# A hybrid decoder trunk on one core: probabilities and the state space output transposed by VectorE in place and by transfers that land in the same tile, with longer steps

## The chip, the core and the metric

The kernel runs on one core of a Trainium2 chip. Its engines work side by side, each through its own instructions in order: TensorE (PE, matmuls and their weight loads PEld), VectorE (DVE), ScalarE (ACT), GpSimd (POOL) and SyncE (SP, which here issues nearly all transfers). The metric is the device time of one execution in microseconds, lower is better. Matmul operands lie in SBUF, results land in PSUM.

## What is computed

Two layers, each: a feed-forward block, a mixer with three branches, a second feed-forward block, on 256 tokens of width 1024 in float32. Cut to what matters here:

```python
def swiglu_ffn(x, w_gu, w_down):                 # FFN_HIDDEN = 2816
    gate, up = jnp.split(x @ w_gu, 2, axis=-1)
    return (jax.nn.silu(gate) * up) @ w_down

def hybrid_mixer(xn, ...):
    q, k, v, z, xbc, dt_raw, u, vg, gate_raw = jnp.split(xn @ w_in, split_at, axis=-1)
    y_a = moba_attention(q, k, v)                # at 256 tokens: causal softmax attention, 8 heads x 128, ALiBi
    y_s = ssd_scan(xs, dt, a, bm, cm) + d_skip[:, None] * xs      # 16 heads x 64, 2 chunks of 128 tokens
    y_s = rms_norm(y_s.reshape(b_, s, SSM_WIDTH) * jax.nn.silu(z), ssm_norm_g)
    y_c = u * spatial_gating(vg)
    merged = gates[:, :, 0] * (y_a @ p_attn) + gates[:, :, 1] * (y_s @ p_ssm) + gates[:, :, 2] * (y_c @ p_sgu)
    return merged @ w_out
...
    h = h + 0.5 * rms_norm(swiglu_ffn(rms_norm(h, g), ...), g2)   # before and after the mixer
```

## The kernel before, in words

**Matmuls.** Every float32 product is made of three matmuls on split operands (hi and lo parts): `x_hi w_hi`, `x_hi w_lo`, `x_lo w_hi` (`unit`, lines 213 to 215). I call these three a triple; one has 512 columns. Weights come in 495 blocks of 128x1024 (512 KB). SP loads a block into one of six `raw` buffers (L160), ScalarE casts it to `whi` (L180), VectorE subtracts to get `wlo` (L181); eleven split pairs are kept. The two tiles of 128 tokens (t = 0, 1) use each block in turn, and a block is two triples wide, so a *step* is two triples and a block is two steps.

**The order.** The order of all instructions is written out by the Python program. After each step `pump` (L198) counts 1.3 off the waiting time of every spawned task, in the order in which they were spawned, lets those that have come to zero go on to their next `yield`, and then emits the next weight split if one is due. The waits stand in the table `W` (L48). A task's wait of 1.3 is one step, one of 5.2 counts down to a tiny positive remainder and takes five, and a wait of 0 lasts until the next step. `finish` lets a task run to its end at once.

**Transposes.** A product needs its left operand with features on partitions. Three ways are in use. `T.transpose` on TensorE, four 128x128 tiles into one PSUM buffer of the tag `tr` (three buffers, `TR`): tokens of q and k (`transposed`, L513, tile `ctr`), the state space output y (`to_parts`, L300, tile `xtr`, then times the gain on VectorE, `xg`, L314) and the probabilities (`attention`, L787, tile `ptr`, copied by ScalarE to `pT`, L789). In the feed-forward part `swap_out` transposes 32x32 squares on VectorE into another tile (L277), writes it to DRAM in one transfer, and `swap_in` reads it back in four transfers that gather pieces of 512 bytes into a third tile `hr` (L286); `evac` waits `W["out"]` between writing and reading and `W["in"]` before it uses the result.

**The mixer around the change.** Projections run in the order xbc, z, q, k, v, gate 1 and the product with `p_ssm`, vg, gate 0 and the product with `p_attn`, u, gate 2 and so on; each half of 512 columns is eight steps. `ssd` (L651) is spawned before the second half of q. For each token tile t and group g it makes decay weights for two sets of four heads: `weights(t, q)` (L676) is one matmul into PSUM (`seg`), a mask added on VectorE (`ssw`, L682), four exponentials on ScalarE (L686), a product on VectorE (L688). `scaled(t)` (L665) starts y on GpSimd (L668) and scales xs on VectorE (L671). Then come the matmuls `yd` (L711), the sum and product into y on VectorE (L714, L722), and at the end of a tile the sum of squares of y on ScalarE (`junk`, L270) and, after `W["ys"]`, `to_parts`. `qk_evac` copies a finished half of q or k from PSUM to `qtok` on ScalarE (L504), waits `W["qk"]` and transposes it on TensorE (`ctr`). `attention` (L746) computes scores and probabilities of one token tile for 8 heads (tiles `sc`), transposes them after `W["p1"]` and multiplies them with v after `W["p3"]` (`pv`, L796). The `branch` product waits for its operand's task by `finish(*need)`.

Of the kernel before, what the change touches and what calls it, by code (L numbers as in the profile page):

```python
# [44 lines left out]
ACC, TR = 5, 3  # L45


W = {'gw': 6.5, 'tr': 0, 'parts': 0, 'sq': 1.3, 'lead': 3.9, 'sq2': 5.2, 'hh': 5.2, 'x0': 0.65, 'cv': 5.2, 'cs': 6.5, 'xs': 0, 'dt1': 2.6, 'dt2': 0, 'dt3': 5.2, 'cb': 2.6, 'w1': 1.3, 'w2': 5.2, 'ys': 3.9, 'qk': 3.9, 'vv': 0, 'qs': 0, 'ex': 0, 'p1': 10.4, 'p2': 0, 'p3': 3.9, 'ge': 0, 'ln': 10.4, 'sv': 0, 'yc': 9.1, 'mg': 3.9, 'out': 6.5, 'in': 6.5}  # L48


@with_exitstack
def trunk(ctx, tc, a):
# [219 lines left out]

    def swap_out(src, w):
        xt = b2("xt")
        V.transpose(xt[:, :w], src[:, :w])  # L277
        rd = dram.tile([P, w], F32, name=f"swap{w}", tag=f"swap{w}", bufs=8)
        nc.sync.dma_start(rd, xt[:, :w])
        return rd  # L280

    def swap_in(dst, rd):

        v = rd.rearrange("(a i) (c e) -> c i a e", a=4, c=4)
        for c in range(4):
            nc.sync.dma_start(dst[32 * c:32 * c + 32], v[c])  # L286

    def halves(ps, hi, lo):

# [105 lines left out]
    def ffn(x, r2, nxt, head=HOLD):  # L395
# [3 lines left out]
        def evac(c, w, gate, up):  # L399
            silu, hh = {}, {}  # L400
            for t in range(NT):
                while gate(t) is None:
                    yield 0
                silu[t] = b2("silu")
                A.activation(silu[t][:, :w], gate(t), AF.Silu, scale=r2[t])  # L405
            for t in range(NT):
                while up(t) is None:
                    yield 0
                hh[t] = b2("hh")
                V.scalar_tensor_tensor(hh[t][:, :w], up(t), r2[t], silu[t][:, :w], op0=ALU.mult, op1=ALU.mult)  # L410
            n = w // P
            rd = {t: swap_out(hh[t], w) for t in range(NT)}
            yield W["out"]
            hr = {}
            for t in range(NT):
                hr[t] = b2("hr")
                swap_in(hr[t][:, :w].rearrange("p (a e) -> p a e", a=4), rd[t])
            yield W["in"]
            new = b4 if n > 2 else b2
            hT[c] = (new("hTh", (P, NT, n, P), F32R), new("hTl", (P, NT, n, P), F32R))  # L420
            for t in range(NT):
                hi, lo = (z[:, t].rearrange("p k (a j) -> p a k j", a=4) for z in hT[c])
                r4 = hr[t][:, :w].rearrange("p (a k j) -> p a k j", a=4, k=n)
# [54 lines left out]
    def mixer(l, x, r2, nxt):  # L478
# [169 lines left out]

        h3 = lambda q, n=SH: q.rearrange("p (h e) -> p h e", h=n)

        def ssd(ysx, rs):  # L651
            bT = lambda g, t: bc["T"][:, g, t * P:(t + 1) * P]
            cT = lambda g, t: bc["T"][:, 2 + g, t * P:(t + 1) * P]
# [38 lines left out]
            for t in range(NT):  # L692
# [53 lines left out]
        def attention(yax, free):  # L746
            for t in range(NT):
                while t and not free:
                    yield 0
                n = (t + 1) * P  # L750
                per = 512 // n
                sc = {}
                mx = small("mx", NH)
                for g in range(2):
                    sc[g] = (b4 if t else b2)("sc", (P, 4, n))
                    for u in range(0, 4, per):
                        ps = tr("qk")
                        for j in range(per):
                            hh = u + j
                            T.matmul(ps[:, j * n:(j + 1) * n], qk["q", g][:, hh, t * P:(t + 1) * P],  # L760
                                     qk["k", g][:, hh, 0:n], start=True, stop=True)
                        for j in range(per):
                            hh = u + j
                            V.scalar_tensor_tensor(sc[g][:, hh, :], alibi[t], 2.0 ** -(4 * g + hh + 1),
                                                   ps[:, j * n:(j + 1) * n], op0=ALU.mult, op1=ALU.add)
                        yield W["qs"]
                    V.reduce_max(mx[:, 4 * g:4 * g + 4], sc[g], axis=AX.X)
                nmx = small("nmx", NH)
                V.tensor_scalar(nmx, mx, -1.0, None, op0=ALU.mult)
                den = small("den", NH)  # L770
                for g in range(2):
                    for j in range(4):
                        c = slice(4 * g + j, 4 * g + j + 1)
                        A.activation(sc[g][:, j, :], sc[g][:, j, :], AF.Exp, bias=nmx[:, c], accum_out=den[:, c])
                    yield W["ex"]
                rden = small("rden", NH)
                V.reciprocal(rden, den)
                for g in range(2):
                    V.tensor_tensor(sc[g], sc[g], rden[:, 4 * g:4 * g + 4, None].to_broadcast([P, 4, n]), op=ALU.mult)
                hi, lo = yax.new(t)  # L780
                for g in range(2):
                    yield W["p1"]
                    pts = {}
                    for k in range(t + 1):
                        pt = tr("ptr")
                        for j in range(4):
                            T.transpose(pt[:, j * P:(j + 1) * P], sc[g][:, j, k * P:(k + 1) * P], ident)  # L787
                        pts[k] = b2("pT", (P, 4, P))
                        A.copy(pts[k], pt.rearrange("p (h q) -> p h q", h=4))  # L789
                        yield W["p2"]  # L790
                    yield W["p3"]
                    po = tr("pv")
                    for j in range(4):
                        hh = 4 * g + j
                        for k in range(t + 1):
                            T.matmul(po[:, j * P:(j + 1) * P], vv[k][:, hh * HD:(hh + 1) * HD], pts[k][:, j, :],  # L796
                                     start=k == 0, stop=k == t)
                    halves(po, hi[:, 4 * g:4 * g + 4, :], lo[:, 4 * g:4 * g + 4, :])


        uu, vg = {}, {}
# [285 lines left out]
def _arrays(i):  # L1087
# [4 lines left out]
    order = [xbc, z, q, k, v, g1, f["p_ssm"], vg, g0, f["p_attn"], u, g2, f["p_sgu"], f["w_out"]]  # L1092
    mix = [_chunks(m).reshape(L, -1, P, 1024) for m in order]
    col = lambda m: m.reshape(L, -1, P).transpose(0, 2, 1)
    par = np.concatenate(
        [col(f["ffn1_pre_g"]), col(f["mix_pre_g"]), col(f["ffn2_pre_g"]), col(f["ssm_norm_g"]),
         f["conv_w"].reshape(L, 4, CT, P).transpose(0, 3, 2, 1).reshape(L, P, 48),
         col(f["conv_b"]), f["sgu_b"].transpose(0, 2, 1)], axis=2)
    return {
# [35 lines left out]
```

## Time and profile before

| what | value |
|---|---|
| median of 3 runs | 1486.92 us (1486.62 to 1488.68) |
| the profiled execution, its own time | 1487.98 us |
| its span, first to last instruction | 1486.2 us |
| TensorE busy | 1472.1 us (99%) |
| VectorE busy | 955.2 us (64%) |
| ScalarE busy | 782.6 us (53%) |
| GpSimd busy | 55.6 us (4%) |
| mean granted TensorE clock | 0.997 |

Busy time is the time in which an engine had an instruction at work; matmuls are pipelined, so the duration of one (about 0.39 us) is longer than the time it adds to a run of them (0.23 us). "Idle before" is the time an engine sat still before an instruction, with the instruction that released it. The granted clock is the share of full speed (2.4 GHz) that TensorE got. Times inside a trace count from the span's start; the two layers show the same pattern some 734.5 us apart, and rows of layer 0 are shown.

### The profile page before, as it was taken

The page shows a single profiled execution, that of the slowest core. Times are in us where ns is not written, and L with a number is a line of the kernel's source. Part 1 is how long each engine was busy: PE and PEld are TensorE (multiplying, and loading weights), DVE is VectorE, ACT ScalarE, POOL GpSimd, SP SyncE. Part 2 cuts the span into 40 slices and gives each one's busy share as a digit, 9 for nine tenths or more (in the row PEclk, how much of TensorE's full clock was granted, in tenths as well). Part 3 has the DMA queues.
Part 4 walks back from the last instruction along what each step waited for, and adds up shares of the span by engine and source line. Part 5 has one row for each costly group of instructions (what it writes and reads, how often), then busy time and mean ns, then how long its engine had stood idle before and what let it go on. Part 6 is the DMA issues. An engine that isn't in the chain of part 4 may idle for free.

```text
span 1486.2 us, 18786 instructions
## 1 busy us (share of the span) xinstructions
PE 1472.1 (99%) x6850; PEld 1218.8 (82%) x6850; DVE 955.2 (64%) x1160; ACT 782.6 (53%) x1079; POOL 55.6 (4%) x98
## 2 busy tenths in 40 slices
PE   9999999999999999999999999999999999999998
PEld 7888888878888888888888888888788888888886
DVE  6766477766666857656486564876665667676652
ACT  6644367555374536544364543765554645464441
POOL 0000020000000000000000000200000000000000
PEclk9999999999999999999999999999999999999999
DMA  8987655335556445888568784654354564478860
GB/s 291 323 253 236 199 190 179 127 115 184 159 181 217 168 154 198 283 230 259 163 230 256 235 253 132 224 167 135 119 192 141 194 204 170 134 272 261 238 200 29
DMA packets 112476, 293.37 MB, mean 197 GB/s; under 512 B 16896, under 2 KB 41600, under 8 KB 112384
## 3 DMA queue, kind: packets, MB, share of 16 engines
q1 hardware_dynamic: 111808, 291.84, 60.6%
q8 instruction: 54, 0.88, 0.2%
q10 hardware_dynamic: 576, 0.33, 0.1%
q14 instruction: 38, 0.31, 0.1%
HBM read 279.54 MB, written 12.58 MB: 197 GB/s over the span
## 4 chain that ended last, share of the span: by engine, by line
PE 94%; DVE 4%; ACT 1%; issue 1%; POOL 0%; DMA 0%; DVEq 0%; ACTq 0%; POOLq 0%
PE gu L213 11%; PE gu L215 11%; PE gu L214 11%; PE dn L213 5%; PE dn L215 5%; PE dn L214 5%; PE br L213 3%; PE br L215 3%; PE br L214 3%; PE gate L215 2%; PE gate L213 2%; PE gate L214 2%; DVE wlo L181 2%; PE xbc L215 1%; PE xbc L213 1%; PE xbc L214 1%
## 5 line engine op out<-in xcount | busy, mean ns | idle before, releaser
L181 DVE TENSOR_TENSOR wlo<-raw,whi 128x1024 fp32r<-128x1024 f32 x495 | 600.2, 1232 | 331.1 <-ACT whi L180 319.8
L180 ACT CAST whi<-raw 128x1024 fp32r<-128x1024 f32 x495 | 512.8, 1051 | 380.9 <-PE gu L215 131.8
L213 PE MATMUL gu<-whi,xh 128*128 128x512 f32 x704 | 276.0, 392 | 1.4 <-ACT xh L316 1.4
L214 PE MATMUL gu<-wlo,xh 128*128 128x512 f32 x704 | 274.9, 391 | 0.0
L215 PE MATMUL gu<-whi,xl 128*128 128x512 f32 x704 | 274.8, 390 | 0.0
L213 PEld LDWEIGHTS gu<-whi,xh 128*128 128x128 f32 x704 | 132.7, 188 | 29.8 <-ACT xh L316 1.8
L215 PEld LDWEIGHTS gu<-whi,xl 128*128 128x128 f32 x704 | 132.6, 188 | 28.0 <-DVE xl L317 0.4
L214 PEld LDWEIGHTS gu<-wlo,xh 128*128 128x128 f32 x704 | 132.5, 188 | 27.9 <-DVE wlo L169 0.9
L213 PE MATMUL dn<-whi,hTh 128*128 128x512 f32 x352 | 137.5, 391 | 0.0
L215 PE MATMUL dn<-whi,hTl 128*128 128x512 f32 x352 | 137.0, 389 | 0.0
L214 PE MATMUL dn<-wlo,hTh 128*128 128x512 f32 x352 | 136.9, 389 | 0.0
L215 PEld LDWEIGHTS dn<-whi,hTl 128*128 128x128 f32 x352 | 66.1, 188 | 13.8
L213 PE MATMUL gate<-whi,xh 128*128 128x512 f32 x192 | 77.3, 403 | 0.0
L214 PEld LDWEIGHTS dn<-wlo,hTh 128*128 128x128 f32 x352 | 66.1, 188 | 13.5
L213 PEld LDWEIGHTS dn<-whi,hTh 128*128 128x128 f32 x352 | 66.1, 188 | 13.4
L215 PE MATMUL gate<-whi,xl 128*128 128x512 f32 x192 | 75.0, 391 | 0.0
L214 PE MATMUL gate<-wlo,xh 128*128 128x512 f32 x192 | 74.8, 390 | 0.0
L316 ACT CAST xh<-xg 128x512 fp32r<-128x512 f32 (+1 forms) x25 | 15.1, 603 | 62.3 <-DVE xg L314 62.3
L215 PEld LDWEIGHTS gate<-whi,xl 128*128 128x128 f32 x192 | 36.0, 188 | 7.7
L405 ACT ACTIVATE silu<-gu,r 128x512 f32<-128x512 f32 (+1 forms) x48 | 31.3, 654 | 19.8 <-PE gu L215 16.2
L214 PEld LDWEIGHTS gate<-wlo,xh 128*128 128x128 f32 x192 | 36.2, 188 | 6.6
L213 PEld LDWEIGHTS gate<-whi,xh 128*128 128x128 f32 x192 | 36.1, 188 | 6.6
(243 smaller groups left out, 2248.3 us busy)
## 6 DMA issues: line engine op xcount, KB each, us to landing
raw<-in_mix SPq DMA_DIRECT2D x232, 512.0 KB, 4.2
raw<-in_gu SPq DMA_DIRECT2D x175, 512.0 KB, 4.9
raw<-in_dn SPq DMA_DIRECT2D x88, 512.0 KB, 4.5
swap<-xt SPq DMA_DIRECT2D x40, 256.0 KB, 3.2
hr<-swap SPq DMA_DIRECT2D x160, 64.0 KB, 4.9
row_ffn_post_g<-in_ffn_post_g SPq DMA_DIRECT2D x4, 512.0 KB, 7.0
swap<-xt SPq DMA_DIRECT2D x8, 128.0 KB, 4.4
hr<-swap SPq DMA_DIRECT2D x32, 32.0 KB, 6.1
```

Source lines behind the costliest of these rows:

```text
L180: A.copy(hi, w)
L181: V.tensor_tensor(lo, w, hi.bitcast(F32), op=ALU.subtract)
L213: T.matmul(o, xh(k, t), hi[:, off:off + n], start=first, stop=False)
L214: T.matmul(o, xh(k, t), lo[:, off:off + n], start=False, stop=False)
L215: T.matmul(o, xl(k, t), hi[:, off:off + n], start=False, stop=last)
L316: A.copy(o_h, xg)
L405: A.activation(silu[t][:, :w], gate(t), AF.Silu, scale=r2[t])
```

## The change

- `swap_out` and `swap_in` give way to `turn` and `land`. `turn` transposes the 32x32 squares in place, then writes to DRAM in four transfers, one per group of 32 partitions, each in pieces (512 bytes; 256 in the chunk of width 256). `land` reads it back in one transfer, whole rows, into the same tile. A transfer of `land` waits for the four writes of its `turn`. The feed-forward part uses them on `hh`; the tiles `xt` and `hr` go.
- The state space output no longer goes through `to_parts`. A task of its own per token tile, `turned`, is spawned with a wait of 1.3 at the tile's end: `turn`, wait `out`, `land`, wait `in`, then gain, cast and subtraction in two halves. `ssd` goes on to the next tile with no wait. `p_ssm` and the gain are stored in the matching order of rows.
- The probabilities are laid out by (32 keys, head, 32 keys) runs: scores are written, reduced, exponentiated and scaled through views of `sc` in runs of 32. `turn` and `land` replace TensorE's transposes and the copies `pT`; between them stand `W["out"]` and then the new `W["pv"]` of 11.7, and `pv` streams `sc` in four runs of 32 columns.
- In `W`, `out` goes from 6.5 to 7.8 and `in` from 6.5 to 9.1, `pv` is new; `ys`, `p1`, `p2`, `p3` are no longer read. `turn_whole` and `land_whole` are added and not called.

```diff
-W = {..., 'ys': 3.9, ..., 'p1': 10.4, 'p2': 0, 'p3': 3.9, ..., 'mg': 3.9, 'out': 6.5, 'in': 6.5}
+W = {..., 'ys': 3.9, ..., 'p1': 10.4, 'p2': 0, 'p3': 3.9, ..., 'mg': 3.9, 'pv': 11.7, 'out': 7.8, 'in': 9.1}
...
+    def turn(src, m, e=128):
+        V.transpose(src, src)
+        rd = dram.tile([m, 4, 32, 4, e], F32, name=f"turn{m}_{e}", tag=f"turn{m}_{e}", bufs=8)
+        for b in range(4):
+            nc.sync.dma_start(rd[:, :, :, b, :].rearrange("m c i e -> i (m c) e"),
+                              src[32 * b:32 * b + 32].rearrange("p (x e) -> p x e", e=e))
         return rd
+    def land(dst, rd):
+        nc.sync.dma_start(dst, rd.rearrange("m c i a e -> (c i) m (a e)"))
...
-            rd = {t: swap_out(hh[t], w) for t in range(NT)}
+            rd = {t: turn(hh[t][:, :w], 1, w // 4) for t in range(NT)}
             yield W["out"]
-            hr = {}
-            for t in range(NT):
-                hr[t] = b2("hr")
-                swap_in(hr[t][:, :w].rearrange("p (a e) -> p a e", a=4), rd[t])
+            for t in range(NT):
+                land(hh[t][:, None, :w], rd[t])
             yield W["in"]
...
+        def turned(t, y, gcol):
+            rd = turn(y, 2)
+            yield W["out"]
+            land(y.rearrange("p (q e) -> p q e", q=2), rd)
+            yield W["in"]
+            new = ysx.new(t)
+            for q in range(2):
+                o_h, o_l = (x[:, 4 * q:4 * q + 4, :].rearrange("p k (a j) -> p a k j", a=4) for x in new)
+                r4 = y[:, 512 * q:512 * q + 512].rearrange("p (a k j) -> p a k j", a=4, k=4)
+                V.tensor_tensor(r4, r4, gcol[:, None, 4 * q:4 * q + 4, None].to_broadcast([P, 4, 4, 32]), op=ALU.mult)
+                A.copy(o_h, r4)
+                V.tensor_tensor(o_l, r4, o_h.bitcast(F32), op=ALU.subtract)
+                yield 0.65
...
                 rs[t] = rsqrt([sumsq(y[t], "sy")], "rs", 1.0 / D)
-                yield W["ys"]
-                yield from to_parts(y[t], *ysx.new(t), gcol=pl[:, G_SSM:G_SSM + 8])
+                yt[t] = spawn(turned(t, y[t], pl[:, G_SSM:G_SSM + 8]), wait=1.3)
...
                 for g in range(2):
-                    V.tensor_tensor(sc[g], sc[g], rden[:, 4 * g:4 * g + 4, None].to_broadcast([P, 4, n]), op=ALU.mult)
+                    V.tensor_tensor(sc[g].rearrange("p (b h j) -> p b h j", h=4, j=32),
+                                    sc[g].rearrange("p (b h j) -> p b h j", h=4, j=32),
+                                    rden[:, None, 4 * g:4 * g + 4, None].to_broadcast([P, 4 * m, 4, 32]), op=ALU.mult)
+                    rd[g] = turn(sc[g], m)
+                    yield 1.3
+                yield W["out"]
+                for g in range(2):
+                    land(sc[g].rearrange("p (m e) -> p m e", m=m), rd[g])
+                yield W["pv"]
                 hi, lo = yax.new(t)
                 for g in range(2):
-                    yield W["p1"]
-                    pts = {}
-                    for k in range(t + 1):
-                        pt = tr("ptr")
-                        for j in range(4):
-                            T.transpose(pt[:, j * P:(j + 1) * P], sc[g][:, j, k * P:(k + 1) * P], ident)
-                        pts[k] = b2("pT", (P, 4, P))
-                        A.copy(pts[k], pt.rearrange("p (h q) -> p h q", h=4))
-                        yield W["p2"]
-                    yield W["p3"]
+                    pts = sc[g].rearrange("p (m a h j) -> p m h a j", m=m, a=4, h=4)
                     po = tr("pv")
...
-        b0 = branch(ysx, rs, [ss], first=True)
+        b0 = branch(ysx, rs, [ss, *yt.values()], first=True)
```

## Rows read from the trace of the kernel before

**Rows 1.** The page's first part: busy time, share of the span and instructions of each engine.

```profile
PE 1472.1 (99%) x6850; PEld 1218.8 (82%) x6850; DVE 955.2 (64%) x1160; ACT 782.6 (53%) x1079; POOL 55.6 (4%) x98
```

**Rows 2.** The page's fourth part: the chain of work that ended last, shares of the span by engine.

```profile
PE 94%; DVE 4%; ACT 1%; issue 1%; POOL 0%; DMA 0%; DVEq 0%; ACTq 0%; POOLq 0%
```

**Rows 3.** Windows of the span, in us from its start: length, then busy time of PE, PEld, DVE, ACT and POOL with their instructions, the granted TensorE clock, the transfers' share and GB/s.

```profile
300.00:315.00 15.00, 12.62 (x57) 9.86 (x56) 10.25 (x11) 7.72 (x14) 2.61 (x3) 0.90 0.29 89
...
400.00:450.00 50.00, 50.00 (x246) 42.02 (x245) 34.12 (x41) 31.22 (x53) 0.00 (x0) 1.00 0.57 190
...
600.00:920.00 320.00, 320.00 (x1422) 265.08 (x1421) 190.81 (x203) 151.47 (x179) 5.08 (x13) 1.00 0.74 231
```

**Rows 4.** What TensorE waited for, over the span: us in total, times, the longest.

```profile
PE ctr L513 <- DVE ssw L682: 3.2, 2, 1.6
PE seg L680 <- DVE xg L314: 1.6, 2, 0.8
```

**Rows 5.** TensorE's timeline in layer 0: start, us, engine, line, operation, tiles, and in brackets the idle time before it and who ended it.

```profile
296.12 1.89 PE L711 MATMUL yd<-xs,ssw 128*128 128x64 f32 x16
297.82 0.48 PE L213 MATMUL k<-whi,xh 128*128 128x512 f32 x1
...
308.72 0.49 PE L680 MATMUL seg<-acsr,sel 128*128 128x512 f32 x1 [0.81 <-DVE xg L314]
310.79 0.63 PE L513 MATMUL ctr<-con,qtok 128*128 128x128 f32 x4 [1.58 <-DVE ssw L682]
...
311.95 0.59 PE L213 MATMUL k<-whi,xh 128*128 128x512 f32 x1
...
315.59 0.39 PE L213 MATMUL k<-whi,xh 128*128 128x512 f32 x1
316.28 0.39 PE L213 MATMUL k<-whi,xh 128*128 128x512 f32 x1
```

**Rows 6.** Windows of one microsecond in that stretch, columns as in rows 3.

```profile
309.00:310.00 1.00, 0.22 (x1) 0.00 (x0) 0.65 (x2) 0.32 (x1) 0.00 (x0) 1.00 0.97 160
...
313.00:314.00 1.00, 1.00 (x3) 0.75 (x3) 1.00 (x2) 0.43 (x1) 0.00 (x0) 0.50 0.00 0
...
315.00:316.00 1.00, 1.00 (x5) 0.82 (x4) 0.62 (x2) 0.34 (x2) 0.00 (x0) 0.80 0.07 4
```

**Rows 7.** TensorE's groups of instructions by line and form over the span: count, busy us, mean ns of one, idle us before them.

```profile
L796 PE MATMUL pv<-pT,v 128*128 128x128 f32 x96 | 12.0, 274 | 0.0
...
L787 PE MATMUL ptr<-con,sc 128*128 128x128 f32 x48 | 7.2, 272 | 0.0
...
L300 PE MATMUL xtr<-con,y 128*128 128x128 f32 x32 | 4.8, 272 | 0.0
```

**Rows 8.** Pieces of the chain that ended last, in order of time: start, us that the piece adds to the chain, engine, tile, line, instructions. There are 8 groups of transposes of y (four per layer) and 12 of the probabilities; one of each is shown, with `yd` and `pv`.

```profile
332.13 1.73 PE yd L711 x16
...
338.91 0.44 PE xtr L300 x4
...
373.42 0.89 PE pv L796 x8
...
1178.22 0.44 PE ptr L787 x4
```

**Rows 9.** Groups of VectorE and ScalarE by line and form: count, busy us, mean ns of one, idle us before them and who ended most of it.

```profile
L277 DVE STREAM_TRANSPOSE xt<-hh 128x512 f32<-128x512 f32 x40 | 25.9, 687 | 0.0
...
L671 DVE TENSOR_TENSOR xs<-xs,dt 128x1024 f32<-128x1024 f32 x4 | 4.9, 1219 | 0.0
...
L424 ACT CAST hTh<-hr 128x512 fp32r<-128x512 f32 x40 | 24.7, 617 | 13.1 <-DMA hr<-swap 12.6 <-issue 0.2
...
L316 ACT CAST xh<-xg 128x512 fp32r<-128x512 f32 x23 | 14.3, 620 | 59.4 <-DVE xg L314 59.4
...
L789 ACT COPY pT<-ptr 128x512 f32<-128x512 f32 x12 | 7.0, 584 | 10.6 <-PE ptr L787 10.6
...
L181 DVE TENSOR_TENSOR wlo<-raw,whi 128x1024 fp32r<-128x1024 f32 x495 | 600.2, 1232 | 331.1 <-ACT whi L180 319.8
```

**Rows 10.** The longest of SP's queue waits over the span: us in total, times, the longest.

```profile
SPq L160 <- DVE wlo L181: 959.2, 416, 17.3
```

**Rows 11.** Transfers by line: count, KB each, median us from issue to landing.

```profile
swap<-xt SPq DMA_DIRECT2D x40, 256.0 KB, 3.2
hr<-swap SPq DMA_DIRECT2D x160, 64.0 KB, 4.9
```

**Rows 12.** Timeline of VectorE, ScalarE and GpSimd at the end of token tile 0 of layer 0, columns as in rows 5.

```profile
298.78 0.69 DVE L722 TENSOR_TENSOR y<-y,zs 128x512 f32<-128x512 f32 x1
...
299.58 1.06 ACT L270 ACTIVATE junk<-y 128x1024 bf16<-128x1024 f32 x1 [3.47 <-DVE y L722]
...
301.58 1.26 ACT L504 ACTIVATE qtok<-k,r 128x512 f32<-128x512 f32 x2
...
301.61 1.90 POOL L668 TENSOR_TENSOR y<-xs,hpar 128x1024 f32<-128x1024 f32 x1
...
301.71 2.89 DVE L181 TENSOR_TENSOR wlo<-raw,whi 128x1024 fp32r<-128x1024 f32 x1 [2.24 <-ACT whi L180]
```

**Rows 13.** ScalarE's exponentials for the first two sets of weights of token tile 0, layer 0, columns as in rows 5.

```profile
275.40 1.28 ACT L686 ACTIVATE ssw<-ssw,nacs 128x128 f32<-128x128 f32 x4 [1.95 <-DVE ssw L682]
...
279.24 1.28 ACT L686 ACTIVATE ssw<-ssw,nacs 128x128 f32<-128x128 f32 x4 [2.08 <-DVE ssw L682]
```

More of the change, by code (lines that the diff above doesn't have):

```diff
@@ L45 @@
 ACC, TR = 5, 3
-W = {'gw': 6.5, 'tr': 0, 'parts': 0, 'sq': 1.3, 'lead': 3.9, 'sq2': 5.2, 'hh': 5.2, 'x0': 0.65, 'cv': 5.2, 'cs': 6.5, 'xs': 0, 'dt1': 2.6, 'dt2': 0, 'dt3': 5.2, 'cb': 2.6, 'w1': 1.3, 'w2': 5.2, 'ys': 3.9, 'qk': 3.9, 'vv': 0, 'qs': 0, 'ex': 0, 'p1': 10.4, 'p2': 0, 'p3': 3.9, 'ge': 0, 'ln': 10.4, 'sv': 0, 'yc': 9.1, 'mg': 3.9, 'out': 6.5, 'in': 6.5}
+W = {'gw': 6.5, 'tr': 0, 'parts': 0, 'sq': 1.3, 'lead': 3.9, 'sq2': 5.2, 'hh': 5.2, 'x0': 0.65, 'cv': 5.2, 'cs': 6.5, 'xs': 0, 'dt1': 2.6, 'dt2': 0, 'dt3': 5.2, 'cb': 2.6, 'w1': 1.3, 'w2': 5.2, 'ys': 3.9, 'qk': 3.9, 'vv': 0, 'qs': 0, 'ex': 0, 'p1': 10.4, 'p2': 0, 'p3': 3.9, 'ge': 0, 'ln': 10.4, 'sv': 0, 'yc': 9.1, 'mg': 3.9, 'pv': 11.7, 'out': 7.8, 'in': 9.1}
 @with_exitstack
@@ L271, in sumsq, with turn_whole, land_whole @@
         return ss
[L275 to L279, printed above, removed]
-        return rd
[L282 to L286, printed above, removed]
+    def turn(src, m, e=128):
[4 more added lines that the diff above has]
+                              src[32 * b:32 * b + 32].rearrange("p (x e) -> p x e", e=e))
+        return rd
+    def land(dst, rd):
+        nc.sync.dma_start(dst, rd.rearrange("m c i a e -> (c i) m (a e)"))
+    def turn_whole(toks):
+        rd = dram.tile([4, P, S], F32, name="turnw", tag="turnw", bufs=6)
+        v = rd.rearrange("k (c i) (t a j) -> t a i (k c) j", c=4, a=4, t=NT)
+        for t in range(NT):
+            V.transpose(toks[t], toks[t])
+            for b in range(4):
+                nc.sync.dma_start(v[t, b], toks[t][32 * b:32 * b + 32, :].rearrange("p (b j) -> p b j", j=32))
+        return rd
+    def land_whole(o, rd):
+        nc.sync.dma_start(o, rd.rearrange("k p e -> p k e"))
     def halves(ps, hi, lo):
@@ L763, in attention @@
                             hh = u + j
-                            V.scalar_tensor_tensor(sc[g][:, hh, :], alibi[t], 2.0 ** -(4 * g + hh + 1),
-                                                   ps[:, j * n:(j + 1) * n], op0=ALU.mult, op1=ALU.add)
+                            V.scalar_tensor_tensor(s4[g][:, hh], alibi[t].rearrange("p (b j) -> p b j", j=32),
+                                                   2.0 ** -(4 * g + hh + 1),
+                                                   ps[:, j * n:(j + 1) * n].rearrange("p (b j) -> p b j", j=32),
+                                                   op0=ALU.mult, op1=ALU.add)
                         yield W["qs"]
-                    V.reduce_max(mx[:, 4 * g:4 * g + 4], sc[g], axis=AX.X)
+                    V.tensor_reduce(mx[:, 4 * g:4 * g + 4], s4[g], axis=AX.XY, op=ALU.max)
                 nmx = small("nmx", NH)
@@ L795, in attention @@
                         for k in range(t + 1):
-                            T.matmul(po[:, j * P:(j + 1) * P], vv[k][:, hh * HD:(hh + 1) * HD], pts[k][:, j, :],
+                            T.matmul(po[:, j * P:(j + 1) * P], vv[k][:, hh * HD:(hh + 1) * HD], pts[:, k, j],
                                      start=k == 0, stop=k == t)
                     halves(po, hi[:, 4 * g:4 * g + 4, :], lo[:, 4 * g:4 * g + 4, :])
+                    yield 1.3
         uu, vg = {}, {}
@@ L1091, in _arrays @@
     q, k, v, z, xbc, dt, u, vg, g0, g1, g2 = (w[:, :, s:e] for s, e in zip(cut[:-1], cut[1:]))
-    order = [xbc, z, q, k, v, g1, f["p_ssm"], vg, g0, f["p_attn"], u, g2, f["p_sgu"], f["w_out"]]
+    weave = lambda m: _woven(np.swapaxes(m, 1, 2), 512).swapaxes(1, 2)
+    order = [xbc, z, q, k, v, g1, weave(f["p_ssm"]), vg, g0, f["p_attn"], u, g2, f["p_sgu"], f["w_out"]]
     mix = [_chunks(m).reshape(L, -1, P, 1024) for m in order]
```

16 lines of the change are left out of this document (10 added, 6 removed).

## The prediction

> **What bounds the kernel now.** I read the page's busy times first: TensorE is busy 1472.1 of 1486.2 us, VectorE 955.2, ScalarE 782.6 [rows 1], and the chain that ended last is 94% TensorE [rows 2]. So a microsecond of TensorE work is a microsecond of the span wherever TensorE has no gap. Then I asked where it has gaps. The windows show 320.00 busy of 320.00 us in the feed-forward stretch and 50.00 of 50.00 in the attention stretch; only 300 to 315 us, inside the mixer, lacks 2.4 us, and its granted clock is 0.90 [rows 3]. TensorE's waits name the culprits, once per layer each: a state space transpose buffer (`ctr` waits for `ssw`, 3.2 us in 2 times; `seg` waits for `xg`, 1.6 us in 2 times) [rows 4]. The timeline shows them at 308.72 (0.81 idle) and 310.79 (1.58 idle); from 311.95 to 315.59 three triples of matmuls take 3.64 us, where one usually takes 0.69 (315.59 to 316.28) [rows 5]. The granted clock is 0.50 there, the lower level (1.2 GHz); it was 1.00 before the two idle gaps and comes back after 315 [rows 6]. 3.64 instead of 2.06 costs 1.6 us. The stretch therefore loses 0.81 + 1.58 + 1.6 = 4.0 us a layer, 8.0 in all.
>
> **Removed from TensorE.** 32 transposes of y and 48 of the probabilities [rows 7] go, in groups of four that take 0.44 us each of the chain [rows 8]: 8 + 12 groups, 20 x 0.44 = **8.8 us off**. TensorE is full there, so this counts whole. Twelve `pT` copies of 584 ns leave ScalarE [rows 9]; nothing of it is on the path.
>
> **Added on VectorE.** Transposes in place: a 512-wide one is 687 ns, and I take 1.22 us for 1024 from the other 1024-wide operation [rows 9]. A layer has two of y (1024), two of 512 and two of 1024 for the probabilities: 6.25 us, 12.5 in all. VectorE is busy 34.12 of 50 us in the attention stretch [rows 3], so this hides behind matmuls; if that cover were gone it would cost 12.5. The new layout in runs of 32 costs nothing that a row shows: ScalarE's cast that gathers such runs (`hTh`) is 617 ns, the plain one (`xh`) 620 [rows 9]. The two groups of PE transposes give their PSUM buffers back to the ring of three.
>
> **The strided moving operand of `pv`.** No row shows one. Nearest: a 64-column `yd` matmul takes as long as a 128-column `pv` one in the chain (1.73 us for 16, 0.89 for 8, both 0.11) [rows 8], so `pv` isn't held by the columns it streams and a slower read has room. It can't gain, as the columns stay. Ends: 0, and 96 [rows 7] x 0.11 = 10.6 us if every one doubled. I take 0, the nearer to that row.
>
> **The transfers.** The feed-forward ones stay ten per chunk, one whole write and four gathers becoming four scattered writes and one whole landing; 60 are new. All go through SP, in order with the weight loads; a landing waits on SP until its four writes are done, and the loads of `raw` queue behind it. SP already spends 959.2 us waiting for VectorE's `wlo` [rows 10], and six raw and eleven split blocks of 2.74 us (two steps) are ahead of TensorE. A scattered write isn't in the trace: 256 KB whole land in 3.2 us, 64 KB in pieces in 4.9 [rows 11]; twice the bytes at most double it, 3.2 to 9.8, and I take 4.9, the row with the same pieces. A step is two triples, 1.37 us. Counting 1.3 off each wait, `out` is now 7 steps (9.6 us), `in` 8 (11.0), `pv` 9 (12.3), so both legs are covered. In the feed-forward part `out` plus `in` grow from 12 to 15 steps; chunk 5 is ready some 17 steps into the `dn` product and first used at the 40th. Cost 0; were it used at once, 3 x 1.37 x 4 = 16 us.
>
> **The moved steps.** This is where I expect something back. Without `ys` and the two `to_parts` halves, `ssd` goes straight on from the first token tile to the second: `weights(1, 0)` and `scaled(1)` come in the step of `yd` at 296.12 [rows 5], `weights(1, 1)` one step later, five steps earlier than now. I walk through it with the rows. VectorE ends y's product at 299.47 and masks `ssw` by 300.1; ScalarE's sum of squares holds it until 300.7 [rows 12]. At token tile 0 the same pair of weights took 5.1 us from the first exponentials (275.40) to the end of the second (279.24 + 1.28) [rows 13], which gives 305.8. But GpSimd's y takes 301.61 to 303.51, and a `wlo` that began at 301.71 lasted 2.89 us [rows 12] instead of 1.23 [rows 9]: the product of `ssw` that follows the first exponentials at 302.0 is held some 1.5 us, 307.3. Behind the second exponentials ScalarE has a `whi` (1.0) and then the first `qtok` of k (0.69): 308.9. Now `qtok` is done at 302.2 because it stands ahead of all that [rows 12]. TensorE needs it at `ctr`, after 297.82 [rows 5] and then two `seg` of 0.23 (a third of a triple) and five steps of 1.37: 305.1. **It waits 3.8 us**, longer than the 0.81 + 1.58 that disappear, and I let the lower clock cost the same 1.6 again: 5.4 a layer, 10.8 in all instead of 8.0, **2.8 us back**. Bounds: the wait may be 0 if the order on ScalarE hides it; at the upper end the step after has `yd`, `yo`, `seg` and `ctr` in a row on three buffers, and `ctr` needs the first add of y, which stands behind one transpose and three `wlo`: 1.3 us more. The lower clock may cost 0 to 3.2, twice what it does now.
>
> **Sum.** -8.8 + 2.8 = -6.0 us. The profiled run took 1487.98 us (span 1486.2 and 1.8 around it), so 1482.0 on its scale; it lies 1.06 above the median of the runs, 1486.92, so **1481.0** for the median.
>
> **Rivals.**
> First, **the stall goes and none comes** (the 4.0 us per layer vanish with the buffers that `xtr` held): -8.8 - 8.0 = -16.8, 1470. For it: both waits name those buffers [rows 4]. Against it: the order on ScalarE just walked.
> Second, **the new stall is at its upper ends**: 2 x (1.3 + 1.6) = 5.8 more, 1486.8, no change. For it: `yd`, `yo`, `seg`, `ctr` in one step; against it: at the lower clock TensorE comes to `ctr` later, so the add of y has time.
> Third, slower: **landings late for `pv`**. If the eight writes of a second-tile step land one after the other at 4.9 us, 39 us, against 9.6 + 12.3 = 21.9 given, TensorE waits 17 us a layer, 34 in all: 1515. It decides from 2.7 us per write on. For it: pieces land slower than whole rows [rows 11]; against it: a write with its 256 KB takes 3.2 from issue, and four gathers overlap now.
> The Trainium skill (DMA: Bandwidth & Descriptors, Rules for kernel authors) advises against splitting one transfer over partition groups, since the parts share the same engines; no run here shows a split write, and by it the four writes would take no less than one whole.
> Fourth, slower: **VectorE becomes the bound**, so that its added 12.5 us lie on the path: -8.8 + 12.5 = +3.7, 1490.6. For it: the same four tiles cost 0.69 us there and 0.44 on TensorE; against it: VectorE's idle third [rows 3, 8, 9].
> The Trainium skill (VectorE: DVE Perf Modes, Rules for kernel authors) advises TensorE for a whole 128x128 transpose whose result may land in PSUM, as VectorE turns only 32x32 blocks; the rows agree on the price per tile (0.44 against 0.69), and by it alone the change would be this fourth rival.
>
> **How the numbers follow.** Forecast 0.47 (1478 to 1483.9), first rival 0.24, second 0.15, third 0.07, fourth 0.07. A measurement here can tell about 0.2%, 3 us, from no change. Faster: 0.47 + 0.24 = 0.71; same 0.15; slower 0.14. The range takes in the forecast, the first rival and the lower part of the second: 1469.5 to 1487.
>
> **What would show it.** Right: no TensorE line that transposes y or the probabilities; stretches of attention still without a gap; one wait of 3 to 4 us per layer of `ctr` for `qtok`, with ScalarE's line order sum of squares, eight exponentials, `whi`, `qtok`, and 0.50 of clock behind it. Wrong: `ctr` without a wait (first rival); `pv` above 0.11 us apiece; TensorE waiting for a landing of `sc` (third); `wlo` named as TensorE's releaser (fourth).

## The result, and the profile after

The changed kernel takes **1495.43 us**, median of 4 runs (1494.57 to 1496.37), beside 1487.63 of the kernel before: a ratio of **1.0053** (95% interval 1.0041 to 1.0065). It is 0.5% slower; the forecast was 1481.0 in a range of 1469.5 to 1487, and the slower side had 14 in 100. The profiled execution took 1494.81 us with a span of 1493.0, 6.8 more than before, at a mean granted clock of 0.992 instead of 0.997.

The page, busy times and shares of the chain that ended last, beside [rows 1, 2]:

```profile
PE 1467.7 (98%) x6770; PEld 1214.9 (81%) x6770; DVE 964.8 (65%) x1172; ACT 776.2 (52%) x1067; POOL 55.6 (4%) x98
...
PE 87%; DVE 7%; ACT 3%; issue 2%; DMA 1%; POOL 0%; ACTq 0%; DVEq 0%; SPq 0%; POOLq 0%
```

80 instructions are gone from TensorE, as foreseen, but its busy time fell by 4.4 us where 8.8 were counted, and the span grew. So TensorE stands still for 25.3 us (1493.0 - 1467.7) where it was 14.1 (1486.2 - 1472.1). TensorE's waits say where, beside [rows 4] (us in total, times, longest):

```profile
PE pv L828 <- DMA sc<-turn: 9.4, 2, 5.3
PE ctr L523 <- ACT qtok L514: 6.7, 2, 3.3
```

Both waits of [rows 4] are gone. In their place stand the wait that the prediction walked out (`ctr` for `qtok`, once per layer) and one that it had costed at nothing: `pv` waits for the landing of the probabilities, once per layer. The windows, columns as in [rows 3], show both places and the one without any change:

```profile
300.00:320.00 20.00, 16.67 (x77) 13.50 (x77) 13.55 (x16) 9.68 (x21) 2.62 (x3) 0.91 0.41 127
...
400.00:450.00 50.00, 45.87 (x209) 38.30 (x208) 34.37 (x42) 27.09 (x46) 0.00 (x0) 0.93 0.67 214
...
600.00:920.00 320.00, 320.00 (x1421) 264.99 (x1420) 190.22 (x203) 152.78 (x180) 4.61 (x11) 1.00 0.73 235
```

The attention stretch, 50.00 busy of 50.00 before, now lacks 4.13 us and has a clock of 0.93; the feed-forward stretch is as full as it was. The account of the span: -8.8 for the transposes, +1.9 for `ctr` (6.7 against 3.2 + 1.6), +9.4 for `pv`, and +4.4 by which the work that stayed on TensorE lasts longer: 6.9, against 6.8 measured. The last term is a difference (8.8 counted, 4.4 seen), not a row. The lower clock accounts for most of it: behind the two waits of `pv` it costs some 2.4 and 1.9 us, as the last section works out, and behind `ctr` as much as behind the old stall (granted 0.66 in the five microseconds from 309.00 here, and in the five from 311.00 before).

**The first wait.** The timeline of the changed kernel at the place of [rows 12]; columns as in [rows 5]:

```profile
301.18 1.26 ACT L713 ACTIVATE ssw<-ssw,nacs 128x128 f32<-128x128 f32 x4
...
302.15 1.91 POOL L695 TENSOR_TENSOR y<-xs,hpar 128x1024 f32<-128x1024 f32 x1
...
302.48 2.13 DVE L715 TENSOR_TENSOR ssw<-ssw,cbt 128x512 f32<-128x512 f32 x1 [1.87 <-ACT ssw L713]
...
306.38 1.28 ACT L713 ACTIVATE ssw<-ssw,nacs 128x128 f32<-128x128 f32 x4 [3.93 <-DVE ssw L709]
...
307.56 1.03 ACT L180 CAST whi<-raw 128x1024 fp32r<-128x1024 f32 x1
...
308.49 1.25 ACT L514 ACTIVATE qtok<-k,r 128x512 f32<-128x512 f32 x2
...
309.23 0.66 PE L523 MATMUL ctr<-con,qtok 128*128 128x128 f32 x4 [3.33 <-ACT qtok L514]
```

This is the order that was forecast: eight exponentials, `whi`, `qtok`, then `ctr`. GpSimd's y (302.15 to 304.06) holds VectorE's product, which lasts 2.13 us for a width that [rows 12] show at 0.69. The Trainium skill (SBUF — State Buffer, SBUF: two separate sides) says that a VectorE operation with two inputs in SBUF and a GpSimd operation that reads SBUF exclude each other for a whole instruction; the trace agrees to 0.14 us, since the product, 0.69 long by itself, ends 0.55 us after GpSimd's operation does.

**The second wait.** The same timeline around the probabilities of the second token tile. SPq rows are transfers as SP issues them; their second number is the time from the first to the last of the group. These are the rows of the kernel after:

```profile
391.55 0.69 DVE L907 TENSOR_TENSOR merged<-br,gate 128x512 f32<-128x512 f32 x1 [10.30 <-PE br L214]
...
406.16 0.39 PE L213 MATMUL vg<-whi,xh 128*128 128x512 f32 x1
...
412.73 1.22 DVE L181 TENSOR_TENSOR wlo<-raw,whi 128x1024 fp32r<-128x1024 f32 x1 [5.05 <-ACT whi L180]
...
415.36 1.25 DVE L277 STREAM_TRANSPOSE sc<-sc 128x1024 f32<-128x1024 f32 x1
...
416.63 4.24 SPq L280 DMA_DIRECT2D turn<-sc  x8
...
417.75 1.25 DVE L277 STREAM_TRANSPOSE sc<-sc 128x1024 f32<-128x1024 f32 x1
...
418.40 0.39 PE L213 MATMUL gate<-whi,xh 128*128 128x512 f32 x1
...
420.97 7.76 SPq L160 DMA_DIRECT2D raw<-in_mix  x4
...
428.83 0.93 SPq L285 DMA_DIRECT2D sc<-turn  x2
...
434.93 3.75 PE L828 MATMUL pv<-sc,v 128*128 128x128 f32 x16 [4.13 <-DMA sc<-turn]
```

TensorE is ready for `pv` at 434.93 - 4.13 = 430.80. The waits in the program put the first write 18 steps before that (one for each of the two `yield 1.3`, 7 for `out`, 9 for `pv`) and the landing 9 steps before it. TensorE passes these two places at 406.16 and 418.40, the `vg` and the `gate` row above. The writes were issued from 416.63 and the landing at 428.83: 10.5 and 10.4 us behind. Of the 12.4 us for the landing 2.0 are left; it takes 6.1 (428.83 to 434.93), and 4.1 are missing. That is the wait.

The lag is there in full at the writes, and it is not made up on the way to the landing. VectorE runs behind TensorE: it stood for 10.30 us at `merged` until the `p_ssm` product ended, and everything queued behind it came late; then it stood for 5.05 us at a `wlo` whose `whi` stands on ScalarE behind the eight exponentials of the probabilities, and the division of the probabilities and their transposes come after that `wlo`. And SP works in order: between the last write and the landing stand four loads of `raw`, which take 7.76 us, of which 6.1 are waits for a `wlo` on VectorE; so SP goes at VectorE's pace. The landing didn't wait for its writes: the last of the eight had landed at 423.25, 5.6 us before the landing was issued. Neither stand of VectorE is work of the change. The kernel before has both in the same places, where nobody waited for them:

```profile
392.28 1.29 DVE L874 TENSOR_TENSOR merged<-br,gate 128x512 f32<-128x512 f32 x2 [10.16 <-PE br L214]
...
413.48 1.23 DVE L181 TENSOR_TENSOR wlo<-raw,whi 128x1024 fp32r<-128x1024 f32 x1 [5.06 <-ACT whi L180]
...
414.85 2.36 DVE L779 TENSOR_TENSOR sc<-sc,rden 128x1024 f32<-128x1024 f32 x2
```

The transfers themselves, from issue to landing, are shorter than the time that the program gives them (kernel after, columns as in [rows 11]):

```profile
turn<-hh SPq DMA_DIRECT2D x160, 64.0 KB, 1.8
hh<-turn SPq DMA_DIRECT2D x40, 256.0 KB, 5.4
...
turn<-y SPq DMA_DIRECT2D x16, 128.0 KB, 2.7
...
turn<-sc SPq DMA_DIRECT2D x16, 128.0 KB, 2.5
sc<-turn SPq DMA_DIRECT2D x4, 512.0 KB, 6.9
```

### The profile page after: what moved, and what is told of

It is laid out like the page before. It is cut to its first block, busy times and chain, and to the rows that moved or that the text cites. A ratio compares the mean times of both kernels' runs of the same rounds, so it can differ in the third digit from the quotient of the medians.

```text
span 1493.0 us, 18572 instructions
## 1 busy us (share of the span) xinstructions
PE 1467.7 (98%) x6770; PEld 1214.9 (81%) x6770; DVE 964.8 (65%) x1172; ACT 776.2 (52%) x1067; POOL 55.6 (4%) x98
## 4 chain that ended last, share of the span: by engine, by line
PE 87%; DVE 7%; ACT 3%; issue 2%; DMA 1%; POOL 0%; ACTq 0%; DVEq 0%; SPq 0%; POOLq 0%
PE gu L213 11%; PE gu L215 11%; PE gu L214 11%; PE dn L215 5%; PE dn L213 5%; PE dn L214 5%; DVE wlo L181 3%; PE br L213 3%; PE br L214 3%; PE br L215 3%; PE gate L213 2%; PE gate L215 2%; PE gate L214 2%; PE xbc L213 1%; PE xbc L215 1%
## 5 line engine op out<-in xcount | busy, mean ns | idle before, releaser
L417 ACT ACTIVATE silu<-gu,r 128x512 f32<-128x512 f32 (+1 forms) x48 | 31.4, 653 | 20.2 <-PE gu L215 16.6
```

## The experiments

All edits below are to the changed kernel. The kernel before, run beside them, had medians of 1487.0 to 1487.31, where it had 1487.63 beside the changed kernel; so a difference to the changed kernel may be off by some 0.6 us. A ratio is the kernel's time over that of the kernel before.

**One part alone.** Three kernels undo parts of the change, to see which of them loses the time.

`e7_attention_undone`: `attention` alone as before.

```diff
-                    rd[g] = turn(sc[g], m)
-                    yield 1.3
-                yield W["out"]
...
-                yield W["pv"]
...
+                    yield W["p1"]
...
+                            T.transpose(pt[:, j * P:(j + 1) * P], sc[g][:, j, k * P:(k + 1) * P], ident)
```

> The changed kernel with attention as before (transposes of the probabilities on TensorE), the state space and feed-forward parts changed. By the sum of the parts: 8 groups of transposes at 0.44 us off (3.5), the old stall of 8.0 replaced by 6.7 of wait and 3.2 of lower clock (1.9 more), so 1487.6 - 3.5 + 1.9 = 1486.0. If the parts act on each other (the probabilities' transposes on VectorE make the stall), the wait of ctr for qtok is gone and it is 1476.

1487.7 us, ratio 1.0001 (0.9992 to 1.001). The wait of `ctr` for `qtok` stays at 6.7, there is no wait of `pv`. Of what the y part saves on TensorE (8 groups, 3.5 us) the longer wait takes back 1.9 (6.7 against 3.2 + 1.6). The remaining 1.6 doesn't show in the time; the interval is as wide (1.5 us either way), so where it went is open.

`e8_y_undone`: the state space output as before, with the order of `p_ssm` and of the gain.

```diff
-                yt[t] = spawn(turned(t, y[t], pl[:, G_SSM:G_SSM + 8]), wait=1.3)
+                yield W["ys"]
+                yield from to_parts(y[t], *ysx.new(t), gcol=pl[:, G_SSM:G_SSM + 8])
...
-    order = [xbc, z, q, k, v, g1, weave(f["p_ssm"]), vg, ...]
+    order = [xbc, z, q, k, v, g1, f["p_ssm"], vg, ...]
```

> The changed kernel with the state space output as before (to_parts on TensorE, p_ssm and gain in the plain order), attention and feed-forward changed. By the sum of the parts: 12 groups at 0.44 us off (5.3), the old stall stays, and the wait of pv with its lower clock (13.8) comes: 1487.6 - 5.3 + 13.8 = 1496.1. If the transposes of y are what puts VectorE behind, the wait of pv is gone and it is 1482.

1494.85 us, ratio 1.0048 (1.0031 to 1.0064). Its TensorE waits:

```profile
PE pv L829 <- DMA sc<-turn: 8.4, 2, 4.3
PE ctr L523 <- DVE ssw L709: 3.1, 2, 1.6
...
PE seg L707 <- DVE xg L326: 1.6, 2, 0.8
```

The waits of [rows 4] are back at their old size, the wait for the landing is there, and the time is that of the whole change. So the loss sits in the probabilities' part, though that part saves 12 groups of transposes (5.3 us).

`e10_ffn_only`: both edits together, so that only the feed-forward part is changed.

> Only the feed-forward part changed (turn and land in place, the longer steps out and in); attention and state space output as before. TensorE has no wait in the feed-forward part before the change, and the result of a chunk is ready some 20 steps before its use: no difference, 1487.0 to 1488.0. Rival (the scattered writes slow the weight loads): over 1490, with whi waiting for raw.

1487.97 us, ratio 1.0001 (0.9992 to 1.0011). The feed-forward part is worth nothing either way, as predicted.

**The wait for the landing.** Three kernels go at it from different ends: later use, earlier readiness, earlier issue.

`e1_pv_later` keeps everything and has `pv` start six steps later.

```diff
-W = {..., 'pv': 11.7, ...}
+W = {..., 'pv': 19.5, ...}
```

> The changed kernel with the wait before the pv product raised from 11.7 to 19.5, six steps (8.2 us) more. In the changed kernel TensorE waits 9.4 us in two times (5.3 and 4.1) for the landing of sc before pv, and I put another 4.4 us of lower clock to it. Theory A (the landing is issued late, because VectorE and with it SP run some 12 us behind TensorE after the product with p_ssm): both waits vanish, 1495.4 - 9.4 - 4.4 = 1481.6. Theory B (the scattered writes and landings are slow in themselves): the same here, since six steps are longer than the longest wait. If the time falls by less than 9 us, something else comes late in its place.

1480.8 us (1478.56 to 1486.38 in 10 runs), ratio 0.9962 (0.995 to 0.9975): 14.6 us less than the changed kernel, with one number. The wait of `pv` is gone, that of `ctr` is unchanged at 6.7. Of the 14.6, 9.4 are the wait itself; the other 5.2 are near the 2.4 + 1.9 us that the lower clock behind the two waits costs.

`e2_merge_later` takes the buffer of `merged` from its pool (`b4`, 16 buffers) only once both halves of the tile's product are done. Before, the instruction stands on VectorE until TensorE's product has read its last operand out of the buffer that `merged` takes over.

```diff
             if first:
+                while (1, t) not in ready:
+                    yield 0
                 merged[t] = b4(f"merged{t}")
```

> The changed kernel with the first merge (the product of p_ssm's result and the gate) emitted when both halves of the result are ready, not at the first; nothing else. In the changed kernel that merge holds VectorE for 10.3 us, because its output buffer comes free only when the product with p_ssm has ended. Theory A (late issue): VectorE no longer stands still there, the transposes of the second tile's probabilities come some 8 to 10 us earlier, the landing is issued by about 421 us instead of 428.8, and the wait of pv shrinks from 9.4 us to under 2: 1482 to 1484. Theory B (slow transfers): the wait stays above 6 us, 1492 to 1495.

1487.81 us, ratio 1.0002 (0.9993 to 1.0011). TensorE's waits and SP's queue in the same stretch:

```profile
PE ctr L523 <- ACT qtok L514: 6.7, 2, 3.3
PE pv L828 <- DMA sc<-turn: 4.1, 2, 2.1
```

```profile
413.86 4.25 SPq L280 DMA_DIRECT2D turn<-sc  x8
...
418.20 7.76 SPq L160 DMA_DIRECT2D raw<-in_mix  x4
...
426.06 0.93 SPq L285 DMA_DIRECT2D sc<-turn  x2
```

The wait falls from 9.4 to 4.1, not below 2 as expected: the writes start 2.77 us earlier (413.86 against 416.63) and the landing with them, but the four loads between still take 7.76. `merged` is one part of the lag, not the whole. VectorE's stand at the `wlo` behind the exponentials is left.

`e6_land_early` leaves the start of `pv` where it is (18 steps after the first write) and puts the landing earlier in the order, so that fewer loads stand ahead of it on SP.

```diff
-                yield W["out"]
+                yield 2.6
                 for g in range(2):
                     land(sc[g].rearrange("p (m e) -> p m e", m=m), rd[g])
-                yield W["pv"]
+                yield 18.2
```

> The changed kernel with the landings of the probabilities emitted two steps after the last write instead of seven, and pv at the same step as before (waits 2.6 and 18.2 for 7.8 and 11.7). In the changed kernel the landings are issued 7.8 us after the last write, because four weight loads stand between them on SP, each waiting for a wlo. Theory A2 (SP's order makes the landing late): it is issued some 5 us earlier, the wait of 9.4 us shrinks to under 2, time 1482 to 1484. Rival (the way from write to landing takes its 14 us whatever stands between): the wait stays above 7 us, 1492 to 1496.

1484.08 us (1480.92 to 1487.93), ratio 0.9981 (0.997 to 0.9992). SP's queue, and TensorE at `pv`:

```profile
416.79 4.24 SPq L280 DMA_DIRECT2D turn<-sc  x8
...
421.12 5.52 SPq L160 DMA_DIRECT2D raw<-in_mix  x2
...
426.74 0.93 SPq L285 DMA_DIRECT2D sc<-turn  x2
...
431.34 2.02 PE L828 MATMUL pv<-sc,v 128*128 128x128 f32 x16 [0.39 <-DMA sc<-turn]
```

The writes are issued when they were (416.79 against 416.63). With two loads between instead of four the landing is issued 2.09 us earlier, not 5 as expected, and the wait still shrinks from 9.4 to 0.8. The rest comes from the landing itself, which reached the first `pv` 4.6 us after its issue (426.74 to 431.34) instead of 6.1; why it was quicker is open. The wait can thus be cured by the place in SP's order although VectorE's lag stays; the writes' own duration is no part of it.

**The wait of `ctr`.** `e3_pause` and `e5_pause5` give back a pause between the two token tiles in `ssd`, of three and of five steps.

```diff
                 yt[t] = spawn(turned(t, y[t], pl[:, G_SSM:G_SSM + 8]), wait=1.3)
+                if t == 0:
+                    yield 3.9        # e5_pause5: 5.2
```

> The changed kernel with a wait of 3.9 (three steps) put back between the first and the second token tile of the state space branch, so that qtok of k stands ahead of the second tile's exponentials on ScalarE. Theory of the moved steps: the wait of ctr for qtok (6.7 us in two times) and the lower clock behind it (about 3.2) go, 1495.4 - 9.9 = 1485.5. Rival (the stall only moves, as the same work meets GpSimd's y and the three PSUM buffers three steps later): 2.4 us of wait per layer stay as before the change, about 1493.5.

1498.92 us, ratio 1.0079 (1.0062 to 1.0096), a miss. The wait didn't go; it moved to the second half of k and grew to 8.2 in 2 times:

```profile
319.36 1.28 ACT L713 ACTIVATE ssw<-ssw,nacs 128x128 f32<-128x128 f32 x4 [4.60 <-DVE ssw L709]
...
323.47 1.28 ACT L713 ACTIVATE ssw<-ssw,nacs 128x128 f32<-128x128 f32 x4 [1.89 <-DVE ssw L709]
...
324.65 1.24 ACT L514 ACTIVATE qtok<-k,r 128x512 f32<-128x512 f32 x2
...
325.38 0.97 PE L523 MATMUL ctr<-con,qtok 128*128 128x128 f32 x4 [4.12 <-ACT qtok L514]
```

The `qtok` of the second half stands behind the later exponentials just as the first one stood behind the earlier. `e4_pause_merge` joins the two edits of `e2` and `e3`.

> Both edits, the later first merge and the three steps between the token tiles. If the two stalls are separate, as theory A and the theory of the moved steps have it, their gains add: 1495.4 - 13.8 - 9.9 = 1471.7, which is 16 us faster than the kernel before the change (20 groups of transposes at 0.44 us, and the 8.0 us of the old stall). If they share a cause (VectorE's load as such), less than 18 of the 23.7 us come.

1490.54 us, ratio 1.0025 (1.0015 to 1.0036): `ctr` 8.2, `pv` 4.7. Only 4.9 of the 23.7 us came, which by its expectation would speak for a shared cause; but `e3` hadn't cured its stall, so it can't tell, and `e9` below can. Two more steps of pause let both `qtok` stand ahead of the exponentials:

> The changed kernel with a wait of 5.2 (five steps) between the two token tiles of the state space branch, where e3 had three. In e3 the wait of ctr for qtok only went from the first half of k to the second (8.2 us in two times), because the second pair of weights of the second tile then came in the step of that half's qtok. Five steps put all of the second tile where the kernel before had it. If ScalarE's order is the cause, both waits of ctr for qtok (6.7 us) and the lower clock behind them (about 3.2) go: 1495.4 - 9.9 = 1485.5. Rival (VectorE is too full here, whatever the order): a wait of 2 us or more per layer remains, of seg or ctr, 1490 or more.

1483.9 us (1482.75 to 1485.53), ratio 0.9976 (0.9967 to 0.9985). No wait of `ctr` is left, `pv` keeps 8.8. So the order on ScalarE is the cause of that wait, and which step the exponentials fall on decides it.

**Both cured.** `e9_all` joins the edits of `e5`, `e2` and `e1`; `e11_pause5_land` joins those of `e5` and `e6`. The comments say which of the two has a line.

```diff
+                if t == 0:
+                    yield 5.2        # both
...
+                while (1, t) not in ready:
+                    yield 0          # e9_all
...
-W = {..., 'pv': 11.7, ...}
+W = {..., 'pv': 19.5, ...}           # e9_all
...
-                yield W["out"]
+                yield 2.6            # e11_pause5_land
...
-                yield W["pv"]
+                yield 18.2           # e11_pause5_land
```

> The changed kernel with the three edits together: five steps between the token tiles (e5), the first merge when both halves are ready (e2) and pv six steps later (e1). e1 alone came to 1480.8 and e5 alone to 1483.9, 14.6 and 11.5 below the 1495.4 of the changed kernel. If the two stalls are separate and nothing else comes late, the gains add: 1469.3, and the profile shows no wait of TensorE in the mixer. That is the first rival of the prediction (1470). If a third thing is late behind them, it stays above 1473.

**1470.69 us** (1470.33 to 1470.73), ratio **0.9886** (0.9871 to 0.9901), 16.6 us below the kernel before: the fastest of the kernels here. No wait of `ctr`, `seg` or `pv` is left. `e1` and `e5` gained 14.6 and 11.5, and together with `e2` they gain 24.7 of these 26.1, so the two stalls are nearly separate. Its page and two of its windows, columns as in [rows 3]:

```profile
PE 1459.3 (99%) x6770; PEld 1209.0 (82%) x6770; DVE 964.8 (66%) x1172; ACT 774.9 (53%) x1067; POOL 55.7 (4%) x98
```

```profile
300.00:320.00 20.00, 20.00 (x100) 16.49 (x99) 15.39 (x16) 11.44 (x21) 2.62 (x3) 1.00 0.60 177
...
400.00:450.00 50.00, 50.00 (x239) 41.95 (x238) 32.76 (x34) 31.76 (x52) 0.00 (x0) 1.00 0.69 220
```

Both stretches are full at a clock of 1.00. VectorE is as busy as in the changed kernel (964.8), so its added work costs nothing here.

> The changed kernel with five steps between the token tiles (e5) and the landings emitted two steps after the last write (e6), pv at the step that the change gave it. e6 alone came to 1484.1, e5 alone to 1483.9: 11.3 and 11.5 below the changed kernel, so 1472.6 if they add, with 0.8 us of wait of pv left. If the landing that now comes earlier on SP delays the weight loads, whi waits for raw more than in the changed kernel and it stays above 1476.

1472.77 us, ratio 0.99 (0.9884 to 0.9917), with 0.9 left of the wait of `pv`. It needs no later `pv`, only an earlier landing, and comes within 2.1 us of `e9`.

`e12_short_ffn_steps` takes `e11` and gives the feed-forward part back its waits of 6.5 and 6.5.

```diff
-            yield W["out"]
+            yield 6.5
...
-            yield W["in"]
+            yield 6.5
```

> e11 with the feed-forward part's waits out and in at 6.5 and 6.5 as before the change (mixer as in e11). The longer steps should be worth nothing there on TensorE's side, since it never waits for this transpose: the same as e11 within 1.5 us, 1472.6. If they are needed, TensorE waits for hTh or hTl, or ScalarE's waits for hh's landing hold the weight splits and the time is 2 us or more above e11.

1472.76 us, ratio 0.9901 (0.9886 to 0.9916). The longer steps are worth nothing there: the work that hides the transfers hid them before.

## Why the prediction was wrong

**The step that failed** is the one on the transfers: "`out` is now 7 steps (9.6 us), `in` 8 (11.0), `pv` 9 (12.3), so both legs are covered ... Cost 0". For `out` and `in` it held (`e10`, `e12`). For `pv` it measured 9.4 us of wait, and with the lower clock behind it 14.6 (`e1`). The step counted TensorE's steps as if the transfers were issued when TensorE passes the place in the program. They are issued when VectorE has done the transpose and SP has done what stands ahead of it; both were behind, by 10.5 us at the writes and by 10.4 at the landing. The same paragraph names the queue ("the loads of `raw` queue behind it") but looks at what queues behind the transfers, not at what stands in front of the landing. `e6` shows what the landing's place in that queue is worth, `e2` shows the part of VectorE's stand at `merged`, `e1` that the wait is the whole difference between slower and faster. Without it `e1` takes 1480.8 us, the forecast 1481.0; that they meet so closely is in part luck, as the runs of `e1` alone spread over 7.8 us.

The signs stood in the trace of before: VectorE standing 10.16 us at `merged` and 5.06 at the `wlo`; the division of the probabilities at 414.85, which ends at 417.21, only 2.7 us before TensorE took up their transposes at 419.91; and SP's 959.2 us of waits for `wlo` [rows 10], which the prediction cites but doesn't read as SP going at VectorE's pace. It read VectorE's share in the stretch [rows 3], 34.12 of 50, and a share doesn't say how late an engine runs.

**The third rival** had the place (landings late for `pv`) and the wrong price and cause. It priced slow writes at up to 39 us and TensorE's wait at 34. The writes landed in a median of 2.5 us, below the 3.2 to 9.8 that the prediction gave them as bounds, and the eight of one step overlapped: they took 6.6 us from the first issue to the last landing (416.63 to 423.25). What was late was their issue. Its point of decision, 2.7 us per write in a row, says nothing of a queue that starts late. The 21.9 us in it are also two steps short: the two `yield 1.3` count too, and the program leaves 18 steps, 24.6 us (406.16 to 430.80).

**The moved steps** were sized rightly where they wait and loosely behind it. Forecast 3.8 us of wait a layer, measured 3.3; `qtok` forecast at 308.2 (308.9 less its own 0.69 where it stands first), read at 308.49; GpSimd's hold of the `ssw` product forecast at 1.5, read at 2.13 - 0.69 = 1.44. The first rival (no stall) is refuted for this kernel by `e7`, and its price is what `e9` reaches with the cures, 1470.69 against 1470, or 16.6 us below the kernel before where the rival says 16.8: without a wait of `ctr`, `seg` or `pv` the 8.8 and the 8.0 are both there to take. Behind the wait the profiled run of the changed kernel lost 5.00 x 0.34 = 1.7 us by its lower clock (0.66), close to the 1.6 forecast; other runs lost more, as the last section shows. The second rival's upper ends (an add of y late for `ctr`) don't appear among TensorE's waits.

**TensorE's 8.8 us** count whole. `e9` takes 12.8 off the busy time (1472.1 - 1459.3), more than 8.8, and the 4.0 above it are near the 3.2 (twice 1.6) that the prediction read for the lower clock behind the old stall [rows 5, 6], which no longer happens (clock 0.999 over the span of `e9`).

**`pv` with a strided operand** costs nothing, the nearer end of the bound. The piece of the chain in the changed kernel, beside [rows 8]:

```profile
379.01 0.89 PE pv L828 x8
```

Eight still add 0.89 us. **VectorE's transposes** were forecast at 1.22 us for 1024 and read at 1.25; the fourth rival (VectorE as the bound) is refuted by the full windows of `e9`, with the same VectorE work. The Trainium skill (VectorE: DVE Perf Modes, Rules for kernel authors) gives whole 128x128 transposes to TensorE where the result may land in PSUM. The rows agree that TensorE is the cheaper engine (0.44 us against 0.69, for four tiles and not, as the prediction says, per tile), and `e9` shows that the dearer engine is the cheaper place when it has idle time and TensorE has none. **The split writes**: a 64 KB part of `hh` lands in a median of 1.8 us, but SP issues the parts one after the other, and from the first issue to the last landing four of them take a median of 3.2 us, as one whole write of 256 KB did [rows 11]. Nothing is gained by the split and nothing lost. The advice of the Trainium skill against splitting (DMA: Bandwidth & Descriptors, Rules for kernel authors) fits that: it says that such parts share the same engines, and here four take no less than one whole.

## What to carry to other kernels

A distance between issue and use that is counted in steps of one engine holds only if the engines that produce and issue keep pace with it: read from the trace, for the very place, when the producer does its last operation before the transfer, and what stands in front of the transfer in its queue. A wait put into an operation's place in the order can be cured from three sides, later use, earlier readiness (which cured about half of it here) and earlier issue, and the cheapest may be a single number. Removing a pause from one task moves its work ahead of others on a shared engine, and the new order should be walked row by row, for the next task too.

## What was not expected of the hardware

**The price of a stall in clock varies.** The same wait of 3.3 us at `ctr` was followed by different clocks. Windows behind it in the profiled run of the changed kernel (first fence) and of `e1_pv_later` (second), columns as in [rows 3]:

```profile
312.00:316.00 4.00, 4.00 (x25) 3.39 (x23) 2.38 (x3) 0.11 (x1) 0.00 (x0) 0.82 1.01 284
316.00:320.00 4.00, 4.00 (x20) 3.30 (x19) 2.52 (x5) 1.63 (x5) 0.00 (x0) 1.00 0.43 173
```

```profile
312.00:316.00 4.00, 4.00 (x19) 3.81 (x19) 1.23 (x1) 0.00 (x0) 0.00 (x0) 0.50 1.02 281
316.00:320.00 4.00, 4.00 (x15) 2.50 (x15) 2.69 (x5) 0.00 (x0) 0.00 (x0) 0.72 0.42 166
```

TensorE is busy for all 4.00 us in each, and the clock is 0.82 in one and 0.50, the lower level of 1.2 GHz, in the other. The runs show it in their times too: `e1`, which keeps this one wait, spreads over 7.8 us in 10 runs, from 1478.56 at a mean clock of 0.998 to 1486.38 at 0.992, while `e9`, without a wait of `ctr`, `seg` or `pv`, spreads over 0.4 us in 4. `e6`, which keeps the wait of `ctr` too, spreads over 7.0 in 10. What decides between the two clocks after equal waits stays open.

**The clock also fell behind the wait for the landing.** In the changed kernel TensorE stood from 430.80 to 434.93, and in layer 1 for 5.25 us until 1173.37:

```profile
430.00:435.00 5.00, 0.87 (x5) 0.44 (x3) 2.90 (x5) 4.09 (x6) 0.00 (x0) 0.79 0.98 340
435.00:440.00 5.00, 5.00 (x21) 4.68 (x22) 4.58 (x5) 3.38 (x6) 0.00 (x0) 0.53 0.96 315
...
1173.30:1178.30 5.00, 4.93 (x22) 4.74 (x23) 3.47 (x4) 2.27 (x5) 0.00 (x0) 0.63 0.96 331
```

The five microseconds behind the first wait were granted 0.53, those behind the second 0.63. By estimate 5.00 x 0.47 = 2.4 and 5.00 x 0.37 = 1.9 us of work at full speed were lost there, behind 9.4 us of waiting.
